# Down products of both feed-forward parts as seven block products for eight, added up in DRAM

## The chip, the core and the metric

The program runs on one core of a Trainium2 chip, as one launch. The metric is device time in microseconds (us) of that launch; lower is better. The engines that matter here are TensorE (PE in the profile; PEld is its weight load), VectorE (DVE), ScalarE (ACT), GpSimd (POOL) and SyncE (SP). SP and POOL issue the DMAs.

## The reference, cut to what matters

One layer of a streaming encoder, all in float32, with x of 1024 rows by 1024 features and a hidden width of 2816:

```python
def swiglu(h, w_gate, w_up, w_down):
    return (jax.nn.silu(h @ w_gate) * (h @ w_up)) @ w_down

    x = x + 0.5 * swiglu(rmsnorm(x, ffn1_norm[l]), ffn1_w_gate[l], ffn1_w_up[l], ffn1_w_down[l])
    x = x + hybrid_mixer(rmsnorm(x, mix_norm[l]), w_in[l], conv_w[l], conv_b[l],
                         sb_out_norm[l], conv_out_norm[l], w_out[l])
    x = x + 0.5 * swiglu(rmsnorm(x, ffn2_norm[l]), ffn2_w_gate[l], ffn2_w_up[l], ffn2_w_down[l])
    return rmsnorm(x, final_norm)
```

The change touches the last product of each `swiglu`, hidden (1024 x 2816) by `w_down` (2816 x 1024), once in part 1, before the mixer, and once in part 2, at the end.

## The kernel before

**Products in three.** A float32 product is made of three matmuls on operands that are split in a high and a low piece (hi by hi, hi by lo, lo by hi). `split` makes the high piece on ScalarE (a copy to the matmul's type, L169) and the low one on VectorE (a subtraction, L170). `mm3` issues the three matmuls, all from L91; one works on a 128 x 128 left tile and 512 columns, and adds up in a bank of PSUM.

**Gate and up.** The hidden tiles (22 of 128 rows, each in two halves of 512 columns) come from units. From tile 2 on a unit makes a tile's two products, gate and up, together as seven block products, named P1, P6, P2, P7, P5, Q4 and P3, in place of eight: the left blocks are combined on VectorE (`left`, L471 to L474), so are the right ones, once, and sums of the results on VectorE give the four blocks (L554 to L565). The hidden tile is written to DRAM, `h_sp`, by a DMA from POOL (L571).

**Down.** Hidden tiles are taken in 11 pairs. Down goes over 14 `TURNS`. A turn has an output tile row g, its partner g + 4, and a window of n pairs (1, 2, 3, then 4 eight times, then 3, 2, 1; 44 in all), so that pairs come and leave one by one while four groups of outputs take turns. In a turn, each pair takes 24 matmuls: two tile rows, two halves, two tiles, three matmuls. `down_prep` of the next turn runs between the products: it splits the pair that is new (1 MB: hidden tiles in part 1, rows of `w_down` in part 2; four splits of 512 columns) and the turn's own columns (rows of the other operand, in tiles named `w`). Both pass through one of two `raw` buffers of 1 MB; `L.load()` issues the next load on SP when one has been taken (L191).

**The flush.** At a turn's end `flush` adds the four banks to tiles of x (part 1, `to_mixer`, L766) or of the residual r (part 2, `to_output`, L1134), four operations on VectorE; these 16 tiles of 128 x 512 stay on chip all through down, after loads in the first four turns (L760, L1128). In the last four turns a tile is done: in part 1 it is fed to the mixer (`act1.feed`: a scaled split at L175 and L176, a running sum of squares at L268 and L269) and written to DRAM, while V, the first projection of the mixer, follows on TensorE; in part 2 the row is normalised (squares on ScalarE L1140, small sums L1143 and L1146, a power on POOL L1151, scaling L1155 and L1157) and written out.

**Order.** The code is written in the order above. The framework's scheduler gives each engine its own sequence and may move instructions ahead of others; waits between engines come from the tiles that they share and from buffers that come round (72 of the tiles named `s`, 10 of `w`, 2 of `raw`, 8 banks of PSUM).

## Time and profile before

| | |
|---|---|
| time, median of three runs | 1918.11 us (1917.59 to 1919.18) |
| time of the profiled execution | 1919.72 us |
| its span | 1918.0 us |
| TensorE busy | 98% of the span, 8440 matmuls |
| VectorE, ScalarE, GpSimd busy | 62%, 40%, 7% |
| TensorE's granted clock, mean | 0.99 |
| data moved by DMA | 187.07 MB, mean 98 GB/s |

The span runs from the first to the last instruction of the profiled execution; its own time stands beside it. An engine's share is an average over stages. In the rows further below a group is a line of the kernel, an engine, an operation and a shape, with its count, busy time and mean, and behind it the engine's idle time just before these instructions and what ended it.

### The profile page before, as it was taken

The numbers are of one execution on the slowest core, as the hardware profiler recorded it, in microseconds if no ns is written. First come the engines' busy times: TensorE is split into PE (matmuls) and PEld (weight loads), VectorE is DVE, ScalarE is ACT, GpSimd is POOL, SyncE is SP. The second block draws the span as 40 slices with busy tenths as digits, with TensorE's granted clock in tenths as the row PEclk, the third lists the DMA queues.
The fourth block names the chain that finished last, engine by engine and source line by source line (L and its number), as shares of the span: only waits on it lengthen the run. The fifth ranks groups of instructions, "written<-read, shape, count | busy, mean of one in ns | idle before, by whom it ended". The sixth has DMA issues, their size and how long they took to land.

```text
span 1918.0 us, 22275 instructions
## 1 busy us (share of the span) xinstructions
PE 1872.8 (98%) x8440; PEld 1549.3 (81%) x8440; DVE 1182.9 (62%) x1829; ACT 770.4 (40%) x1366; POOL 133.0 (7%) x238
## 2 busy tenths in 40 slices
PE   6989999999999999999999999999999999999997
PEld 5768888888888888888888877877888888888886
DVE  4896555655543258577788798679555656554324
ACT  4543222222321046466687785634223232232113
POOL 1100000000000011110101000200000000000001
PEclk8989999999999999999999999999999999999999
DMA  7123222223742032422313324303222322464202
GB/s 236 50 73 97 84 86 80 88 77 101 249 155 83 17 120 90 94 64 63 92 49 77 97 83 154 132 22 110 77 88 77 93 72 94 133 219 137 83 28 77
DMA packets 206907, 187.07 MB, mean 98 GB/s; under 512 B 8608, under 2 KB 174544, under 8 KB 206800
## 3 DMA queue, kind: packets, MB, share of 16 engines
q1 hardware_dynamic: 190160, 140.55, 24.4%
q0 software_dynamic: 16640, 45.10, 7.3%
q8 instruction: 66, 1.08, 0.2%
q14 instruction: 41, 0.34, 0.1%
HBM read 133.46 MB, written 42.73 MB: 92 GB/s over the span
## 4 chain that ended last, share of the span: by engine, by line
PE 91%; DVE 5%; issue 1%; ACT 1%; DMA 1%; SPq 0%; POOL 0%; POOLq 0%; DVEq 0%; ACTq 0%
PE ps L91 89%; DVE s L170 1%; DMA raw<-in_ffn_w_gate 1%; DVE w L170 1%; DVE s L269 0%; DVE s L496 0%; PE ps L277 0%; DVE s L595 0%; DVE s L176 0%; PE ps L853 0%; DMA s<-in_x 0%; SPq L677 0%; ACT w L169 0%; PE ps L683 0%; DVE s L875 0%
## 5 line engine op out<-in xcount | busy, mean ns | idle before, releaser
L91 PE MATMUL ps<-s,w 128*128 128x512 f32 x6880 | 1623.1, 391 | 25.9 <-ACT s L175 11.7
L91 PEld LDWEIGHTS ps<-s,w 128*128 128x128 f32 x6880 | 1286.0, 189 | 294.2 <-ACT s L175 12.6
L169 ACT CAST w<-raw 128x1024 fp32r<-128x1024 f32 (+3 forms) x182 | 181.1, 996 | 493.8 <-PE ps L91 339.6
L170 DVE TENSOR_TENSOR w<-raw,w 128x1024 fp32r<-128x1024 f32 (+3 forms) x182 | 209.2, 1151 | 138.4 <-ACT w L169 80.1
L91 PE MATMUL ps<-s,s 128*128 128x512 f32 (+3 forms) x704 | 179.0, 375 | 2.0 <-DVE s L170 1.0
L91 PEld LDWEIGHTS ps<-s,s 128*128 128x128 f32 x704 | 132.0, 188 | 29.3 <-DVE s L170 1.8
L170 DVE TENSOR_TENSOR s<-raw,s 128x512 fp32r<-128x512 f32 x128 | 85.0, 684 | 56.0 <-ACT s L169 56.0
L169 ACT CAST s<-raw 128x512 fp32r<-128x512 f32 x128 | 74.6, 617 | 85.0 <-DMA raw<-in_ffn_w_down 46.7
L566 ACT ACTIVATE s<-s 128x512 f32<-128x512 f32 x40 | 25.3, 633 | 202.8 <-DVE s L565 202.8
L766 DVE SCALAR_TENSOR_TENSOR s<-ps,s 128x512 f32<-128x512 f32 x56 | 38.0, 688 | 97.7 <-PE ps L91 97.3
L1134 DVE SCALAR_TENSOR_TENSOR s<-ps,s 128x512 f32<-128x512 f32 x56 | 37.9, 687 | 93.5 <-PE ps L91 93.4
L571 POOL DMA_DIRECT2D h_sp<-s x80 | 43.2, 539 | 742.7 <-DVE s L570 742.6
L551 ACT ACTIVATE s<-ps 128x512 f32<-128x512 f32 x40 | 23.8, 598 | 133.0 <-PE ps L91 133.0
L170 DVE TENSOR_TENSOR w<-w,w 128x1024 fp32r<-128x1024 f32 x40 | 49.0, 1224 | 41.2 <-PE ps L91 39.0
L471 DVE TENSOR_TENSOR w<-raw 128x1024 f32<-128x1024 f32 x40 | 48.8, 1223 | 34.6 <-PE ps L91 34.6
L554 DVE TENSOR_TENSOR s<-s,ps 128x512 f32<-128x512 f32 x40 | 27.4, 686 | 66.2 <-PE ps L91 66.2
L1007 DVE TENSOR_TENSOR s<-s,ps 128x128 f32<-128x128 f32 (+2 forms) x96 | 52.6, 548 | 16.8 <-ACT s L1003 16.4
L995 ACT ACTIVATE s<-ps 128x128 f32<-128x128 f32 (+2 forms) x96 | 47.0, 489 | 37.8 <-PE ps L91 37.5
L557 DVE TENSOR_TENSOR s<-s,ps 128x512 f32<-128x512 f32 x40 | 27.4, 686 | 56.3 <-PE ps L91 56.3
L170 DVE TENSOR_TENSOR s<-s,s 128x512 fp32r<-128x512 f32 x88 | 58.4, 682 | 5.6 <-ACT s L169 5.5
L1003 ACT ACTIVATE s<-s 128x128 f32<-128x128 f32 (+2 forms) x96 | 50.2, 523 | 20.6 <-DVE s L999 19.3
L169 ACT CAST s<-s 128x512 fp32r<-128x512 f32 x88 | 51.0, 618 | 18.5 <-DVE s L328 7.7
(122 smaller groups left out, 1451.8 us busy)
## 6 DMA issues: line engine op xcount, KB each, us to landing
h_sp<-s POOLq DMA_DIRECT2D x88, 256.0 KB, 2.3
raw<-in_ffn_w_gate SPq DMA_DIRECT2D x43, 512.0 KB, 3.9
raw<-in_ffn_w_up SPq DMA_DIRECT2D x43, 512.0 KB, 5.2
raw<-h_sp SPq DMA_DIRECT2D x11, 1024.0 KB, 5.0
raw<-in_ffn_w_down SPq DMA_DIRECT2D x11, 1024.0 KB, 4.8
raw<-in_w_in SPq DMA_DIRECT2D x20, 512.0 KB, 3.7
s<-s POOLq DMA_DIRECT2D x72, 128.0 KB, 2.4
x_sp<-s POOLq DMA_DIRECT2D x32, 256.0 KB, 2.3
```

The costliest lines, as they stand in the source:

```text
L91: nc.tensor.matmul(out, lhs, rhs, **kw)
L169: nc.scalar.copy(hi, x)
L170: nc.vector.tensor_tensor(out=lo, in0=x, in1=f(hi), op=ALU.subtract)
L471: nc.vector.tensor_tensor(out=two(y), in0=two(blk(1, 2)), in1=blk(3).unsqueeze(1).to_broadcast([P, 2, HALF]), op=ALU.add)
L554: nc.vector.tensor_tensor(out=self.u2, in0=self.p1, in1=o, op=ALU.subtract)
L557: nc.vector.tensor_tensor(out=self.u3, in0=self.u2, in1=self.o[2], op=ALU.add)
L571: nc.gpsimd.dma_start(out=self.out[:, hs(hf)], in_=u)
L766: nc.vector.scalar_tensor_tensor(out=x, in0=o[hf], scalar=0.5, in1=x, op0=ALU.mult, op1=ALU.add)
L995: behind(nc.scalar.activation(u["s"][:, cols], u["z"][:, cols], AF.Exp), table_set)
L1003: nc.scalar.activation(sc, sc, AF.Ln, bias=1.0)
L1007: nc.vector.tensor_tensor(out=sc, in0=sc, in1=u["z"][:, cols], op=ALU.max)
L1134: nc.vector.scalar_tensor_tensor(out=r, in0=o[hf], scalar=0.5, in1=r, op0=ALU.mult, op1=ALU.add)
```

## The change

Down becomes seven block products for eight in both parts, on the plan that gate and up had before. `h_sp` goes. In its place `Aside` takes hidden tiles as they are made and writes seven combinations for each pair of tiles to DRAM, `c_sp`: three are halves of the tiles as they stand, four are sums or differences; four operations on VectorE a pair (L637) and seven puts of 256 KB from POOL. In part 1 these are the right blocks and come back ready (`right_back`, L729), while the columns of `w_down` are combined into left blocks by `left`, now with a width. In part 2 they are the left blocks (`left_back`, L506: seven loads a turn, in rows of 128 columns), and the right ones are combined from rows of `w_down` (`right_rows`).

A turn runs the seven products in the order P1, P6, P2, P7, P5, Q4, P3, each n pairs deep: 21 matmuls a pair in place of 24. P1 and P2 share a bank, P7 and Q4, P5 and P3, so the second of each waits until the first has been taken out. The windows are now 2, 3, 4, 4, 3, 3, 3, 4, 4, 4, 4, 3, 2, 1 pairs, 44 as before. The first ten turns add four results each onto x or r in DRAM, by DMAs from POOL that accumulate (`add`, L795); one sum u stays on chip for each g (L805, L808). The last four turns load x or r back (four loads of 256 KB a turn) and add the results and u to it on VectorE (`end`, L835). The factor of a half is now in the hidden tile.

The diff, cut to its core (the parts on loads of weights and on the normalisation are left out):

```diff
--- before.py
+++ after.py
-    h_sp = [dr.tile([NF, P, S], F32, name=f"h_sp{i}") for i in range(2)]
...
-    TURNS = [(i % 4, max(0, i - 3), min(NQ, i + 1)) for i in range(NQ + 3)]
+    FACTORS = ("P2", "P1", "P3", "P6", "P7", "P5", "Q4")
+    c_sp = [dr.tile([7, NQ, P, HALF], F32, name=f"c_sp{i}") for i in range(2)]
+    UPTO = (2, 3, 4, 4, 5, 6, 7, 8, 9, 10) + (NQ,) * 4
+    TURNS = [(i % 4, UPTO[i - 4] if i > 3 else 0, n) for i, n in enumerate(UPTO)]
...
-    def left(raw):
+    def left(raw, n=HALF):
...
+    def left_back(g, q0, q1):
+        a = {}
+        n = (q1 - q0) * P
+        def load(to, i):
+            nc.sync.dma_start(out=to.rearrange("p (k c) -> p k c", c=P),
+                              in_=c_sp[1][i, q0:q1, :, g * P : (g + 1) * P].rearrange("k p c -> p k c"))
+        yield a
+        for i in (0, 2, 4):
+            raw = w4(F32)[:, : 2 * n]
+            for j in range(2):
+                load(raw[:, j * n : (j + 1) * n], i + j)
+            parts = split(w4()[:, : 2 * n], w4()[:, : 2 * n], raw)
+            for j in range(2):
+                a[FACTORS[i + j]] = tuple(x[:, j * n : (j + 1) * n] for x in parts)
+            yield
+        raw = s()[:, :n]
+        load(raw, 6)
+        a["Q4"] = split(s(F32R)[:, :n], s(F32R)[:, :n], raw)
...
+    class Blocks:
...
+        def product(self, name):
             i = BANK[name]
             first = i not in self.o
             if first:
                 self.o[i] = bank()
             o = self.o[i]
-            for k in range(4):
-                run(mm3(o, wk(self.a[name], k), self.b[name][k], first and k == 0,
-                        k == 3 and name in ("P2", "P6", "Q4", "P3"), skip_group_check=True))
+            for k in range(self.n):
+                run(mm3(o, wk(self.a[name], k), self.b(name, k), first and k == 0,
+                        k == self.n - 1 and name in ("P2", "P6", "Q4", "P3"), skip_group_check=True))
             self.done.add(name)
+            return o
...
+    class Aside:
...
+        def take(self, m, hf, x):
+            j, odd = divmod(m, 2)
+            if not odd:
+                if not hf:
+                    self.e0 = x
+                    self.put(j, 0, x)
+                else:
+                    self.e1 = x
+                    self.t1 = self.comb(s(), self.e0, x, self.op)
+                    self.put(j, 1, self.t1)
+            elif not hf:
+                self.o0 = x
+                self.put(j, 2, x)
+            else:
+                self.put(j, 3, x)
+                t2 = self.comb(s(), self.t1, x, ALU.add)
+                self.put(j, 5, t2)
+                t3 = self.comb(self.e1, x, self.e1, self.op)
+                self.put(j, 4, t3)
+                t4 = self.comb(s(), t2, self.o0, self.op)
+                self.put(j, 6, t4)
...
+    def right_back(q):
+        b = ring[q] = {}
+        def load(name):
+            raw = s()
+            nc.sync.dma_start(out=raw, in_=c_sp[0][FACTORS.index(name), q])
+            return raw
+        raw = load(FEW[0])
+        for i, name in enumerate(FEW):
+            now, raw = raw, load(FEW[i + 1]) if i < 6 else None
+            b[name] = split(s(F32R), s(F32R), now)
             yield
+    def right_rows(q):
+        b = ring[q] = {}
+        raw, _ = L.take()
...
+        done("P1", b11)
+        comb(b11, b11, b12, ALU.subtract)
+        t2 = comb(s(), b11, b22, ALU.add)
+        yield
+        done("P6", t2)
+        yield
+        done("P2", b21)
+        comb(b21, t2, b21, ALU.subtract)
+        yield
+        done("P7", comb(b12, b22, b12, ALU.subtract))
+        yield
+        done("P5", b11)
+        yield
+        done("Q4", b21)
+        yield
+        done("P3", b22)
         L.load()
-    def down(flush, start=None):
+        yield
+    def down_prep(i, j):
+        g, q0, q1 = TURNS[j]
+        steps = [left_back(g, q0, q1) if i else left(L.take()[0], (q1 - q0) * P)]
+        lefts[j] = next(steps[0])
+        steps += [(right_rows if i else right_back)(q) for q in news(j)]
+        while steps:
+            for x in list(steps):
+                if next(x, steps) is steps:
+                    steps.remove(x)
+            yield
+    class Turn(Blocks):
...
+        def add(self, i, hf, x):
+            nc.gpsimd.dma_start(out=self.acc(self.g + 4 * i, hf), in_=x, accum_op=ALU.add)
+        def do(self, name, ready):
+            o = self.product(name)
+            if name == "P1":
+                if self.first:
+                    self.kept[self.g] = s()
+                    nc.scalar.copy(self.kept[self.g], o)
+                else:
+                    u = self.kept[self.g]
+                    nc.vector.tensor_tensor(out=u, in0=u, in1=o, op=ALU.add)
+            if name == "P6":
+                u = self.kept[self.g]
+                nc.vector.tensor_tensor(out=u, in0=u, in1=o, op=ALU.subtract)
+            if self.last:
+                self.end(name, o, ready)
+                return
+            if name == "P2":
+                x = s()
+                nc.scalar.copy(x, o)
+                self.add(0, 0, x)
+            if name == "P7":
+                self.p7 = s()
+                nc.scalar.activation(self.p7, o, AF.Copy, scale=-1.0)
+            if name == "P5":
+                nc.vector.tensor_tensor(out=self.p7, in0=self.p7, in1=o, op=ALU.subtract)
+                self.add(1, 1, self.p7)
+            if name == "Q4":
+                x = s()
+                nc.scalar.activation(x, o, AF.Copy, scale=-1.0)
+                self.add(1, 0, x)
+            if name == "P3":
+                x = s()
+                nc.scalar.copy(x, o)
+                self.add(0, 1, x)
+        def end(self, name, o, ready):
+            x = lambda i, hf: self.tiles(self.g + 4 * i, hf)
+            def comb(t, y, op):
+                nc.vector.tensor_tensor(out=t, in0=t, in1=y, op=op)
+            if name == "P6":
+                u = self.kept.pop(self.g)
+                comb(x(0, 1), u, ALU.add)
+                comb(x(1, 1), u, ALU.subtract)
+                comb(x(1, 0), u, ALU.subtract)
+            if name == "P2":
+                comb(x(0, 0), o, ALU.add)
+                ready(self.g, 0)
+            if name == "P7":
+                comb(x(1, 1), o, ALU.subtract)
+            if name == "P5":
+                comb(x(1, 1), o, ALU.subtract)
+                ready(self.g + 4, 1)
+            if name == "Q4":
+                comb(x(1, 0), o, ALU.subtract)
+                ready(self.g + 4, 0)
+            if name == "P3":
+                comb(x(0, 1), o, ALU.add)
+                ready(self.g, 1)
+    def down(i, acc, tiles, back, ready):
         for j, (g, q0, q1) in enumerate(TURNS):
-            prep = down_prep(j + 1) if j + 1 < len(TURNS) else iter(())
-            if start:
-                start(j)
-            last = j >= NQ - 1
-            for i in range(2):
-                o = [bank(), bank()]
-                n = (q1 - q0) * 2
-                for k in range(n):
-                    hi, lo = (a[:, k * P : (k + 1) * P] for a in rows_of[j][i])
-                    for hf in range(2):
-                        run(mm3(o[hf], (hi, lo), ring[q0 + k // 2][k % 2, hf], k == 0, k == n - 1))
-                    if k % 2:
-                        next(prep, None)
-                flush(j, g, i, o)
+            prep = down_prep(i, j + 1) if j + 1 < len(TURNS) else iter(())
+            if j + 1 >= NQ - 1 and j + 1 < len(TURNS):
+                for hf in range(2):
+                    back((j + 1) % 4, hf)
+                    back((j + 1) % 4 + 4, hf)
+            turn = Turn(j, acc, tiles)
+            for name in FEW:
+                turn.do(name, ready)
+                next(prep, None)
             run(prep)
         ring.clear()
-        rows_of.clear()
+        lefts.clear()
     x_in = t["x"][0]
...
-    def x_back(j):
-        if j < 4:
-            for i in range(2):
-                for hf in range(2):
-                    d = j + 4 * i
-                    nc.sync.dma_start(out=xT(d, hf), in_=x_sp[0][d][:, hs(hf)])
-
-    def to_mixer(j, g, i, o):
-        d = g + 4 * i
-        for hf in range(2):
-            x = xT(d, hf)
-            nc.vector.scalar_tensor_tensor(out=x, in0=o[hf], scalar=0.5, in1=x, op0=ALU.mult, op1=ALU.add)
-            if j >= NQ - 1:
-                act1.feed(d, hf, x, x)
-                nc.gpsimd.dma_start(out=x_sp[1][d][:, hs(hf)], in_=x)
-
-    down(to_mixer, x_back)
+    def x_back(d, hf):
+        nc.sync.dma_start(out=xT(d, hf), in_=x_sp[0][d][:, hs(hf)])
+    def to_mixer(d, hf):
+        x = xT(d, hf)
+        act1.feed(d, hf, x, x)
+        nc.gpsimd.dma_start(out=x_sp[1][d][:, hs(hf)], in_=x)
+    down(0, lambda d, hf: x_sp[0][d][:, hs(hf)], xT, x_back, to_mixer)
...
```

How the change moves instructions, at three places. The first is VectorE in the last turn but one and the last turn of part 1's down. In before, four flushes a turn alternate with the mixer's feed (L176) and sums (L269):

```order
L176 SCALAR_TENSOR_TENSOR s_4982<-s_3416,gains_495,s_4981 128x512
L766 SCALAR_TENSOR_TENSOR s_3481<-ps_4992,s_3481 128x512
L176 SCALAR_TENSOR_TENSOR s_4988<-s_3418,gains_495,s_4987 128x512
L766 SCALAR_TENSOR_TENSOR s_3483<-ps_4993,s_3483 128x512
L269 TENSOR_TENSOR s_4716<-s_4716,s_5004 128x512
L269 TENSOR_TENSOR s_4718<-s_4718,s_5007 128x512
L176 SCALAR_TENSOR_TENSOR s_5014<-s_3481,gains_495,s_5013 128x512
L766 SCALAR_TENSOR_TENSOR s_3485<-ps_5024,s_3485 128x512
L176 SCALAR_TENSOR_TENSOR s_5020<-s_3483,gains_495,s_5019 128x512
```

In the changed kernel the same place, around the first products of the last turn (`s_3746` is the sum u, `ps_5565` the bank of P1 and P2, `ps_5570` that of P6, `ps_5590` that of P7 and Q4, `ps_5598` that of P5 and P3):

```order
L805 TENSOR_TENSOR s_3746<-s_3746,ps_5565 128x512
L269 TENSOR_TENSOR s_5231<-s_5231,s_5572 128x512
L808 TENSOR_TENSOR s_3746<-s_3746,ps_5570 128x512
L835 TENSOR_TENSOR s_5446<-s_5446,ps_5565 128x512
L835 TENSOR_TENSOR s_5450<-s_5450,s_3746 128x512
L835 TENSOR_TENSOR s_5452<-s_5452,s_3746 128x512
L835 TENSOR_TENSOR s_5448<-s_5448,s_3746 128x512
L176 SCALAR_TENSOR_TENSOR s_5586<-s_5446,gains_495,s_5585 128x512
L269 TENSOR_TENSOR s_5278<-s_5278,s_5592 128x512
L835 TENSOR_TENSOR s_5452<-s_5452,ps_5590 128x512
L170 TENSOR_TENSOR w_5652<-raw_5410,w_5651 128x1024
L835 TENSOR_TENSOR s_5452<-s_5452,ps_5598 128x512
```

Ten evictions and adds stand where four flushes stood, and the feed of a tile (L176) follows only when its last add is made; in part 2 the same adds stand before the normalisation.

The second place is SP's queue at the start of part 2's down in the changed kernel (`raw` are rows of `w_down`, `c_sp_80` the combinations; x2 marks two alike):

```order
L191 DMA raw_13659<-in_ffn_w_down 128x2x1024
L191 DMA raw_13793<-in_ffn_w_down 128x2x1024
L506 DMA w_13844<-c_sp_80 128x2x128 x2
L506 DMA w_13879<-c_sp_80 128x2x128 x2
L506 DMA w_13908<-c_sp_80 128x2x128 x2
L506 DMA w_14051<-c_sp_80 128x3x128 x2
L506 DMA s_13940<-c_sp_80 128x2x128
L506 DMA w_14073<-c_sp_80 128x3x128 x2
L191 DMA raw_14030<-in_ffn_w_down 128x2x1024
L191 DMA raw_14036<-in_ffn_w_down 128x2x1024
```

The third load of down weights, `raw_14030`, stands behind the left loads of turn 0 and the first of turn 1, and there are two `raw` buffers. In before, the second operand's loads went through `raw` too.

The third place is TensorE's sequence at the start of part 1's down in the changed kernel (`ps_3736`, `ps_3760`, `ps_3803` and `ps_3825` are turn 1's banks of P1, P6, P7 and P5, `ps_3607` is turn 0's bank of P1 and P2):

```order
L91 MATMUL ps_3736<-s_3417,w_3616 128x512
L91 MATMUL ps_3736<-s_3418,w_3616 128x512
L91 MATMUL ps_3736<-s_3417,w_3617 128x512
L91 MATMUL ps_3760<-s_3441,w_3655 128x512
L91 MATMUL ps_3760<-s_3442,w_3655 128x512
L91 MATMUL ps_3803<-s_3502,w_3674 128x512
L91 MATMUL ps_3760<-s_3441,w_3656 128x512
L91 MATMUL ps_3760<-s_3447,w_3655 128x512
...
L91 MATMUL ps_3803<-s_3503,w_3674 128x512
L91 MATMUL ps_3825<-s_3537,w_3674 128x512
L91 MATMUL ps_3825<-s_3538,w_3674 128x512
L91 MATMUL ps_3607<-s_3471,w_3401 128x512
L91 MATMUL ps_3607<-s_3472,w_3401 128x512
```

Products of turn 1 stand ahead of turn 0's P2; in before the turns followed one another there as they are written.

## Rows read from the trace of the kernel before

**Rows 1.** The page: span, engines' busy time, the chain that ended last.
```profile
span 1918.0 us, 22275 instructions
...
PE 1872.8 (98%) x8440; PEld 1549.3 (81%) x8440; DVE 1182.9 (62%) x1829; ACT 770.4 (40%) x1366; POOL 133.0 (7%) x238
...
PE 91%; DVE 5%; issue 1%; ACT 1%; DMA 1%; SPq 0%; POOL 0%; POOLq 0%; DVEq 0%; ACTq 0%
```

**Rows 2.** Windows, down at 482:726, 1670:1910; us, busy (count), PEclk, DMA share, GB/s.
```profile
97.00:470.00 373.00, 367.29 (x1602) 302.46 (x1601) 238.34 (x311) 112.43 (x157) 20.50 (x38) 0.99 0.28 84
482.00:726.00 244.00, 244.00 (x1078) 202.06 (x1077) 108.29 (x152) 66.66 (x100) 9.63 (x20) 1.00 0.38 123
1285.00:1660.00 375.00, 370.41 (x1627) 304.83 (x1628) 236.04 (x307) 115.30 (x163) 20.50 (x38) 1.00 0.27 84
1670.00:1910.00 240.00, 236.27 (x1043) 195.31 (x1041) 100.50 (x160) 58.76 (x104) 7.83 (x9) 1.00 0.36 115
```

**Rows 3.** Groups by form, 482:726 us, down of part 1.
```profile
L766 DVE SCALAR_TENSOR_TENSOR s<-ps,s 128x512 f32<-128x512 f32 x56 | 38.0, 688 | 97.7 <-PE ps L91 97.3
L170 DVE TENSOR_TENSOR w<-raw,w 128x1024 fp32r<-128x1024 f32 x21 | 25.6, 1222 | 11.8 <-ACT w L169 11.8
L170 DVE TENSOR_TENSOR s<-raw,s 128x512 fp32r<-128x512 f32 x39 | 25.4, 684 | 22.9 <-ACT s L169 22.9
...
L169 ACT CAST s<-raw 128x512 fp32r<-128x512 f32 x38 | 21.5, 616 | 38.3 <-DMA raw<-h_sp 38.3
...
L176 DVE SCALAR_TENSOR_TENSOR s<-s,gains,s 128x512 fp32r<-128x512 f32 x15 | 10.8, 745 | 0.0
...
L269 DVE TENSOR_TENSOR s<-s,s 128x512 f32<-128x512 f32 x12 | 7.7, 683 | 0.0
...
L170 DVE TENSOR_TENSOR w<-raw,w 128x768 fp32r<-128x768 f32 x4 | 3.8, 956 | 3.3 <-ACT w L169 3.3
...
L170 DVE TENSOR_TENSOR w<-raw,w 128x256 fp32r<-128x256 f32 x2 | 0.8, 416 | 0.0
```

**Rows 4.** Timeline from 690 us, end of part 1's down: start, us, instruction.
```profile
719.71 9.23 PE L91 MATMUL ps<-w,s 128*128 128x512 f32 x40
...
729.33 1.05 PE L277 MATMUL ps<-ones_r,s 128*128 128x1 f32 x8 [0.39 <-DVE s L269]
```

**Rows 5.** Timeline from 1885 us, the kernel's end.
```profile
1884.80 21.47 PE L91 MATMUL ps<-s,w 128*128 128x512 f32 x94
...
1908.85 0.15 DVE L1146 SCALAR_TENSOR_TENSOR sm<-sm,sm 128x1 f32<-128x1 f32 x1
...
1909.08 0.92 POOL L1151 TENSOR_TENSOR sm<-sm,mhalf 128x1 f32<-128x1 f32 x1 [2.30 <-DVE sm L1146]
1910.04 0.72 ACT L1157 ACTIVATE s<-s,sm 128x512 f32<-128x512 f32 x1 [1.28 <-POOL sm L1151]
1910.04 0.49 DVE L1155 TENSOR_SCALAR s<-s,sm 128x512 f32<-128x512 f32 x1 [0.44 <-POOL sm L1151]
```

**Rows 6.** Groups by form, 200:455 us, gate and up of part 1.
```profile
L471 DVE TENSOR_TENSOR w<-raw 128x1024 f32<-128x1024 f32 x13 | 15.9, 1225 | 14.0 <-PE ps L91 14.0
...
L473 DVE TENSOR_TENSOR raw<-w,raw 128x512 f32<-128x512 f32 x13 | 8.9, 684 | 0.0
```

**Rows 7.** DMA issues: count, KB each, median us to landing.
```profile
h_sp<-s POOLq DMA_DIRECT2D x88, 256.0 KB, 2.3
...
raw<-in_ffn_w_down SPq DMA_DIRECT2D x11, 1024.0 KB, 4.8
...
s<-x_sp SPq DMA_DIRECT2D x32, 256.0 KB, 5.1
raw<-in_ffn_w_down SPq DMA_DIRECT2D x16, 512.0 KB, 5.3
raw<-h_sp SPq DMA_DIRECT2D x16, 512.0 KB, 5.8
```

**Rows 8.** Timeline from 455 us, SP's queue.
```profile
474.68 1.92 SPq L760 DMA_DIRECT2D s<-x_sp  x4
```

More of the change, by code (lines that the diff above doesn't have):

```diff
@@ L386, in ffn_weights @@
             yield [part(j * S, w[:, m * P : (m + 1) * P]) for j, w in enumerate((wg, wu))]
[L387 to L388 removed]
         for j, (g, q0, q1) in enumerate(TURNS):
[L390 to L393 removed]
+            if i:
+                for q in news(j):
+                    yield [part(0, wd[2 * q * P : 2 * (q + 1) * P])]
+                continue
+            n = (q1 - q0) * P
+            rows = wd[2 * q0 * P : 2 * q1 * P].rearrange("(k two p) c -> two p k c", two=2, p=P)
+            yield [(b * n, n, (lambda a: a.rearrange("p (k c) -> p k c", c=P)),
+                    rows[two, :, :, d * P : (d + 1) * P])
+                   for b, (two, d) in enumerate(((1, g), (0, g), (1, g + 4), (0, g + 4)))]
     def mixer_weights():
@@ L601, in gate_up @@
         preps = [left(L.take()[0]) for _ in range(2)]
-        units = [Unit(next(p), b, out[nstd + j]) for j, p in enumerate(preps)]
+        units = [Unit(next(p), b, out(nstd + j)) for j, p in enumerate(preps)]
         for p in preps:
@@ L616, in gate_up @@
         for m in range(nstd + 2, NF):
-            unit = Unit(a, b, out[m])
+            unit = Unit(a, b, out(m))
             if m + 1 < NF:
@@ L621, in gate_up @@
             else:
-                prep = down_prep(0)
+                prep = down_prep(i, 0)
             for name in FEW:
@@ L626, in gate_up @@
             run(prep)
-    ring, rows_of = {}, {}
-    def down_prep(j):
-        if j < NQ:
-            raw, _ = L.take()
-            ring[j] = {}
-            for i in range(4):
-                ring[j][divmod(i, 2)] = split(s(F32R), s(F32R), raw[:, hs(i)])
-                yield
-            L.load()
-        raw, n = L.take()
-        rows_of[j] = []
-        for i in range(2):
-            c = slice(i * n // 2, (i + 1) * n // 2)
-            rows_of[j].append(split(w4()[:, : n // 2], w4()[:, : n // 2], raw[:, c]))
-            yield
-        L.load()
@@ L647, in down @@
[L647 to L663 removed]
+    ring, lefts = {}, {}
@@ new lines, in right_back, with comb, done @@
+    def right_back(q):
[8 more added lines that the diff above has]
+            b[name] = split(s(F32R), s(F32R), now)
+            yield
+    def right_rows(q):
+        b = ring[q] = {}
+        raw, _ = L.take()
+        b11, b12, b21, b22 = (raw[:, i * HALF : (i + 1) * HALF] for i in range(4))
+        def comb(out, x, y, op):
+            nc.vector.tensor_tensor(out=out, in0=x, in1=y, op=op)
+            return out
+        def done(name, x):
+            b[name] = split(s(F32R), s(F32R), x)
+        done("P1", b11)
[14 more added lines that the diff above has]
+        done("P3", b22)
+        L.load()
+        yield
@@ new lines, in down_prep, with __init__ @@
+    def down_prep(i, j):
[7 more added lines that the diff above has]
+                    steps.remove(x)
+            yield
+    class Turn(Blocks):
+        kept = {}
+        def __init__(self, j, acc, tiles):
+            self.g, q0, q1 = TURNS[j]
+            super().__init__(lefts[j], lambda name, k: ring[q0 + k][name], q1 - q0)
+            self.first, self.last = q0 == 0, q1 == NQ
+            self.acc, self.tiles = acc, tiles
+        def add(self, i, hf, x):
+            nc.gpsimd.dma_start(out=self.acc(self.g + 4 * i, hf), in_=x, accum_op=ALU.add)
+        def do(self, name, ready):
+            o = self.product(name)
+            if name == "P1":
[52 more added lines that the diff above has]
+                ready(self.g, 1)
```

128 lines of the change are left out of this document (69 added, 59 removed).

## The prediction

> **What bounds the kernel now.** I read first the shares of the engines and the chain of work that ended last: TensorE is busy 98% of the 1918.0 us, and 91% of the chain is TensorE [rows 1]. Then the stretches the change touches, by windows: in both down products TensorE is busy 240 to 244 us of 240 to 244, at a granted clock of 1.00, with VectorE at 108 and 100 us, ScalarE at 67 and 59 and the DMA engines at 0.36 to 0.38 [rows 2]. So down waits for nothing but its own matmuls, and a matmul costs 244.00/1078 = 0.2263 us in part 1 and 236.27/1043 = 0.2265 in part 2: 0.2264 us. Grouped by form, VectorE's flushes idle 97.3 us behind TensorE [rows 3]; it has room on the mean. Last the two ends. After the last down product of part 1 TensorE runs 40 matmuls of the V projection, and the next product that needs VectorE starts 0.39 us after them [rows 4]: the handover is covered almost exactly. At the kernel's end the last matmul stops at 1884.80 + 21.47 = 1906.27, and the last normalisation at 1910.76 [rows 5].
>
> The profiled execution took 1919.72 us for the span of 1918.0; the median of the three runs is 1918.11, so I sum on the profile and take 1.6 off at the end. These three differ by 1.6 us; 0.2% (3.8 us) is about what a measurement tells from no change: faster is below 1914.3, slower above 1921.9.
>
> **Removed.** Down of a part had 14 turns with 24 matmuls per pair of hidden tiles, 44 pair-turns: 1056. Seven products for eight make 21, so 924. Two parts save 264 matmuls: 264 × 0.2264 = **−59.8 us**. That is all if TensorE stays fed. A turn of n pairs is then 4.75 n us and one product 0.68 n us; down of a part falls from 239 to 209 us. The 112 flushes of 0.688 us [rows 3] go too, but they were hidden.
>
> **Added, and hidden in the middle.** Counting the order's VectorE instructions in down of part 1 at the durations of [rows 3] gives some 185 us in 210, in the middle turns 77 to 80%; ScalarE some 110. Neither binds on the mean; both bind where work is bunched, which is at the ends of the two downs. Four combinations of 512 columns per pair are added on VectorE in gate_up, 0.684 each as the row of that shape has it [rows 6], 2.7 us per pair of 38 us, where VectorE now runs 238.34/373 = 64% [rows 2]: 72%, hidden under TensorE but for jitter, **+1** (0 to 2). The three puts more per pair are POOL's and not waited for.
>
> **End of part 1's down.** The four end turns add onto the residual on VectorE: ten operations a turn, as the order piece on VectorE shows, plus the feeding of the mixer. Between the eviction of P1 of turn 12 and that of P5 of turn 13 (P3 shares its bank and waits) VectorE has 36 instructions: 18 evictions and adds at 0.686, 6 feeds at 0.745, 6 sums at 0.683, splits of 1.222, 2 × 0.416 [rows 3], and three of 128 columns, by the slope (0.684 − 0.416)/256 an estimated 0.28 each: 12.4 + 4.5 + 4.1 + 1.2 + 0.8 + 0.8 = 23.8 us. TensorE has 54 matmuls and five of V that stand ahead: 59 × 0.2264 = 13.4. It waits **+10.4**. The last V matmuls behind hide the rest as now [rows 4]. Bounds: 6, if the earlier work is drawn forward, and 14.
>
> **End of part 2's down.** The same stretch: 24 adds and scalings of 0.686, six small ones at 0.15, three scalings at 0.49 [rows 5], splits 3 × 0.416 + 0.28 [rows 3]: 20.4 us against 54 × 0.2264 = 12.2, so 8.2 late. In return the last chain, 4.5 us from the last matmul on [rows 5], loses one flush of two, since P3's half row alone is left behind it: about 0.7 to 0.9 less. Net **+7.5** (4 to 11).
>
> **Start of part 1's down.** The left factors of turn 1 are built in tiles that the last unit's P3 frees. From there to the split that gives P3 and P6 of turn 2 the order has 31 VectorE instructions: eleven splits of 512 columns at 0.684, two of 768 at 0.956, two of 1024 at 1.222, three operations of 384 columns at 0.55 (on the same slope), two combinations of 768 and 1024 at 0.96 and 1.23 [rows 3, 6], and eleven combinations and evictions of 512 columns at 0.686: 23.2 us, against 85 matmuls or 19.2. So 4.0 late; the shuffling of turns 0 and 1, seen in the order piece on TensorE, is counted in the 85. The transfers say much the same: the last unit and turns 0 and 1 carry 28 loads of 7.3 MB, left columns of 2.4, puts of 1.3 and adds of 2.1, 13.1 MB in 42.8 us, 306 GB/s; the present stretches move 84 at a share of 0.28, 123 at 0.38 and 115 at 0.36, so 300 to 324 when all engines work [rows 2]. That just fits, up to 1 late; adds counted twice make 15.2 MB, 50.7 us at 300, 8 late. I take **+6** (3.6 to 10.6, both waits in part).
>
> **Start of part 2's down.** There are two raw buffers. As the order piece on SP shows, the third load of down weights stands behind the left loads and waits for a buffer: it is free only after pair 0's last split, 7.8 us of VectorE after the last unit's Q4 starts. Then come 4.8 for 1 MB [rows 7], a cast of 0.62 and a subtraction of 0.69 [rows 3]: 4.4 late for turn 1's P1, 6.2 for its P6. **+6.5** (4 to 10). The loads of the residual are moved from the turns 0 to 3 to the turns 10 to 13; on SP each takes 0.48 us of issue [rows 8], four a turn, in turns of 14 to 19 us: nothing.
>
> **Adds in DRAM.** Forty DMAs per part of 256 KB, issued by POOL at 0.54 us each, add onto DRAM. No row shows one. From below a plain write of 256 KB, landed in 2.3 us; from above its read and write, 5.1 + 2.3 = 7.4 [rows 7]. No engine waits for one but for its buffer, a turn later; what counts is the DMA engines' time. In part 1 a turn of three pairs (14.3 us) moves 1.8 MB of right blocks, 0.8 of left and 1.05 of adds: 3.7 MB, 12.2 us at 300 GB/s; adds counted twice make 4.7 MB, 15.7 us, 1.4 late in each of three turns. Turns of four pairs have 19.0 us for 13.1 or 16.6; part 2 carries 5% less. **+2** (0 to 7) for both parts, nearer the read-and-write bound, since an add must do both.
>
> The Trainium skill, "DMA: Bandwidth & Descriptors", section "Bandwidth", speaks against this: transfers of 64 KB reach 138 GB/s and one should batch to 1 MiB, and part 2's left factors now come in loads of 128 to 256 KB with rows of 512 bytes. In the trace 512-byte rows cost little: 512 KB, issued in pairs, land in 5.3 and 5.8 us, 1 MB in long rows in 4.8 [rows 7]. At 138 GB/s throughout, a turn of three pairs in part 2 would take an estimated 25 us for 14.3; by the rows 12.
>
> **Sum.** −59.8 + 1 + 10.4 + 7.5 + 6 + 6.5 + 2 = −26.4: 1919.7 − 26.4 = 1893.3, on the median 1891.7; I write **1893**, since small waits at the seams are likelier missed than double counted.
>
> **Rivals.**
> A, the forecast: the give-backs of 33 us, each with its own bounds, come to 18 at the lowest and 55 at the highest; together 22 to 45 are likely: 1880 to 1903. 0.62.
> B, the ends are filled: two thirds of the 30 us at the four ends vanish, since work is pulled forward into them (five V matmuls and the shuffled turns show that the order does it): −59.8 + 12 = −48, so 1870 (1865 to 1880). For it: VectorE idles 97 us in a down now [rows 3]. Against: at the ends its work hangs on the products just made. 0.15.
> C, the other side: the DMA engines become the bound in down. At four plain writes for an add, a turn of three pairs carries 2.6 + 4.2 = 6.8 MB, 23 us for 14.3, one of four 7.1 MB, 24 for 19: 3 × 8 + 3 × 5, and turns 0 to 2 some 25 more, 62 a part, of which buffers absorb perhaps a third: −26 + 2 × 41 = +56, 1974. At three writes the same sum gives 5 us, 1 us and 8 in those turns, 26 a part, two thirds of it 17: −26 + 34 = +8. So it decides from about three plain writes an add. For it: no row prices an add. Against: a read and a write land in 7.4, which is 3.2 of 2.3 but mostly time of travel [rows 7]. 0.12. In its section "Rules for kernel authors" the page named above says that an accumulating DMA reads its destination and writes it later, so that another write between is lost and each must wait for the one before; adds to one block stand four turns apart here, so that alone costs nothing.
> D, the change keeps next to nothing: each end at its upper bound gives back 45 to 60, so 1903 to 1921. 0.08.
> E, part 2's left loads, now in rows of 512 bytes and 128 to 256 KB, move slowly. At a quarter of 300 GB/s a turn of three pairs takes 3.5/0.3 = 11.6 us, and 7.9 more for its 0.8 MB: 19.5 for 14.3; one of four 12.5 and 10.5 more, 23 for 19: 3 × 5 + 4 × 4, 31 us, 1912 to 1925; at a half it all fits. For it: each turn has seven such loads. Against: such rows land in 5.3 to 5.8 us for two of 512 KB together [rows 7]. 0.03. That is the mechanism of the page's rule on 64 KB, at a rate below its 138.
>
> **Chances.** Faster is A, B and 0.04 of D: 0.81; same the rest of D and 0.02 of E: 0.06; slower C and the rest of E: 0.13. The range leaves out C, E, a third of D and a sliver of B, 0.2 in all: 1868 to 1914.
>
> **What the profile after would show.** TensorE with 264 matmuls fewer, still 0.226 us each, and in four places stalls: before P3 of the last turn of part 1's down with VectorE as releaser (about 10 us), the same at the kernel's end (8), at turn 1 of part 1 behind a split or a c_sp load (6), at turn 1 of part 2 behind a load of down weights (6). The middle turns show TensorE at over 97%; a plain write and an adding one would differ in time to landing by at most 5 us. I am wrong if the middle turns stall with DMA as releaser (C), if the stalls at the ends add up to less than 12 (B), or if gate_up takes over 3 us more.

## The result, and the profile after

The changed kernel takes 1949.24 us (median of four runs, 1944.06 to 1956.14), before 1918.64 (1917.59 to 1919.99): 1.0161 times as long, 95% interval 1.0126 to 1.0196. That is 31 us longer, well outside the scatter of the runs, where 25 us less were forecast. The profiled execution took 1946.61 us; its span is 1944.9, 26.9 more than before, and the accounts below are made on it.

The page after: the span, the engines' busy time and count, and the two DMA queues with packets, MB and the time of their packets as a share of 16 engines.

```profile
span 1944.9 us, 23049 instructions
...
PE 1845.2 (95%) x8176; PEld 1506.7 (77%) x8176; DVE 1384.8 (71%) x2145; ACT 887.6 (46%) x1576; POOL 238.2 (12%) x384
...
q1 hardware_dynamic: 216720, 157.87, 26.8%
q0 software_dynamic: 33440, 83.38, 16.6%
```

Against [rows 1]: 8440 − 8176 = 264 matmuls are gone, as planned, and TensorE's share of the span fell from 98% to 95%. The second queue, POOL's, stood at this in before:

```profile
q0 software_dynamic: 16640, 45.10, 7.3%
```

Where the time went is read off TensorE's timeline. The product Q4 has both operands in tiles `s`, so in the timeline it stands out as `ps<-s,s`. From the order of TensorE's instructions I count the matmuls between two such marks; at 0.2264 us each they give the time that TensorE needs, and what the trace has beyond that is lost. Here are the marks in the changed kernel: the last unit but one of gate and up, turns 3, 11 and 13 of part 1's down, the mixer's first sum (L277); then the same of part 2 without the sum. Below, the start of a down is what lies between the unit's mark and turn 3's, the middle runs from turn 3 to turn 11, and the end is the rest.

```profile
460.01 2.88 PE L91 MATMUL ps<-s,s 128*128 128x512 f32 x12
...
549.62 2.88 PE L91 MATMUL ps<-s,s 128*128 128x512 f32 x12
...
699.06 2.20 PE L91 MATMUL ps<-s,s 128*128 128x512 f32 x9
...
724.68 1.62 PE L91 MATMUL ps<-s,s 128*128 128x512 f32 x3 [4.58 <-DVE s L835]
...
737.13 1.05 PE L277 MATMUL ps<-ones_r,s 128*128 128x1 f32 x8
...
1659.48 2.88 PE L91 MATMUL ps<-s,s 128*128 128x512 f32 x12
...
1760.10 2.88 PE L91 MATMUL ps<-s,s 128*128 128x512 f32 x12
...
1905.28 2.20 PE L91 MATMUL ps<-s,s 128*128 128x512 f32 x9
...
1933.27 1.65 PE L91 MATMUL ps<-s,s 128*128 128x512 f32 x3 [1.74 <-DVE s L835]
```

Between the first two marks stand 357 matmuls, 80.8 us; the trace has 89.6, so 8.8 are lost at the start of part 1's down. From turn 3 to turn 11 it is 594 matmuls, 134.5 us, for 149.4: 15.0 lost in the middle. Part 2 has the same counts: 100.6 for 80.8, 19.8 lost at its start, and 145.2 for 134.5, 10.7 in its middle. The sum at L277 stood at 729.33 in before [rows 4], so part 1 as a whole lost 7.8; its unit of 460.01 stood at 455.87, so 4.1 of these were gone before down began. From L277 to the unit of 1659.48 are 922.35 us, in before 912.94: 9.4 more are lost ahead of part 2's down. The mixer in between took 0.2 more, so they belong to gate and up. The ends are not measured by themselves: they are what is left of the 26.9. All of it beside the forecast, in us:

| step of the prediction | forecast | in the trace |
|---|---|---|
| matmuls removed | −59.8 | −59.8 |
| gate and up (both) | +1 | +13.5 |
| start of part 1's down | +6 | +8.8 |
| middle turns of both parts, adds in DRAM | +2 | +25.7 |
| end of part 1's down | +10.4 | +9.8 |
| start of part 2's down | +6.5 | +19.8 |
| end of part 2's down, net | +7.5 | +9.1 |
| sum | −26.4 | +26.9 |

The middle turns. The issues of DMAs, with count, KB each and median us to landing:

```profile
s<-c_sp SPq DMA_DIRECT2D x83, 256.0 KB, 6.4
x_sp<-s POOLq DMA_DIRECT2D x72, 256.0 KB, 4.1
...
raw<-in_ffn_w_down SPq DMA_DIRECT2D x11, 1024.0 KB, 7.7
```

40 of the 72 writes to `x_sp` add, and the median of all is 4.1 us where plain ones took 2.3; the 1 MB load, 4.8 in [rows 7], takes 7.7. What follows from late loads is seen at 590 us, in turn 6 (start, us, engine, instruction, idle time before and its releaser):

```profile
592.42 6.53 SPq L729 DMA_DIRECT2D s<-c_sp  x7
...
600.14 0.62 ACT L169 CAST s<-s 128x512 fp32r<-128x512 f32 x1 [8.90 <-DMA s<-c_sp]
...
600.79 0.69 DVE L170 TENSOR_TENSOR s<-s,s 128x512 fp32r<-128x512 f32 x1 [6.66 <-ACT s L169]
...
603.23 0.51 PE L91 MATMUL ps<-s,w 128*128 128x512 f32 x1 [3.36 <-ACT s L169]
```

Seven loads are issued in a burst; ScalarE stands 8.90 us before the first has landed, with casts and evictions queued behind; VectorE waits for ScalarE and TensorE for both. The DMA engines are full in that burst and nearly idle after it (us, busy and count of PE, PEld, DVE, ACT, POOL, then the granted clock, DMA share, GB/s; a share over 1 says that packets' times overlap):

```profile
594.00:598.00 4.00, 4.00 (x19) 3.30 (x19) 0.14 (x1) 0.00 (x0) 0.00 (x0) 1.00 1.12 262
...
602.00:606.00 4.00, 1.75 (x4) 1.24 (x5) 4.00 (x5) 4.00 (x7) 0.58 (x1) 0.82 0.11 39
```

The start of part 2's down, on SP, ScalarE and TensorE:

```profile
1693.22 1.84 SPq L191 DMA_DIRECT2D raw<-in_ffn_w_down  x2
...
1700.16 0.62 ACT L169 CAST s<-raw 128x512 fp32r<-128x512 f32 x1 [8.05 <-DMA raw<-in_ffn_w_down]
...
1700.83 1.95 PE L91 MATMUL ps<-s,w 128*128 128x512 f32 x3 [4.14 <-ACT s L169]
```

The third load of down weights goes out at 1693.22, when the raw buffer is free, and lands 6.9 us later. The left loads (L506) were held back too: in this stretch (1660 to 1715 us) SP stood 32.0 us, in six waits, until TensorE had read tiles `w` that they were to overwrite.

```profile
SPq L506 <- PE ps L91: 32.0, 6, 8.3
```

After the stall three matmuls take 1.95 us, not 0.68. The windows show the clock that TensorE was granted:

```profile
710.00:730.00 20.00, 13.21 (x45) 9.51 (x45) 19.75 (x33) 9.22 (x14) 4.24 (x8) 0.76 0.44 147
1700.00:1720.00 20.00, 15.69 (x49) 10.61 (x50) 11.50 (x17) 9.92 (x17) 3.50 (x4) 0.74 0.85 201
...
1701.00:1710.00 9.00, 6.24 (x12) 3.44 (x13) 5.67 (x9) 4.02 (x7) 0.90 (x1) 0.50 0.80 206
...
1920.00:1940.00 20.00, 9.87 (x29) 6.25 (x28) 15.61 (x35) 8.07 (x21) 3.69 (x4) 0.72 0.30 105
530.00:670.00 140.00, 130.40 (x558) 104.86 (x559) 88.57 (x123) 67.51 (x112) 26.84 (x31) 0.99 0.79 201
```

After the 4.14 us in which TensorE stood before 1700.83, it was granted 0.50 of its clock from 1701 to 1710: the lower level, 1.2 GHz of 2.4. In 1700 to 1720 it is busy 15.69 us for 49 matmuls, 4.6 more than 49 × 0.2264. And at the end of part 1's down VectorE is busy 19.75 us of 20 and TensorE 13.21: that is the wait that was worked out ahead.

Gate and up. At the start of part 2's, on VectorE, first before (L170 on `s<-s` splits the right factors, L579 ends the second hidden tile), then after (L671 and L637 are that tile and its combinations):

```profile
1271.36 1.28 DVE L170 TENSOR_TENSOR s<-s,s 128x512 fp32r<-128x512 f32 x2
...
1278.69 1.28 DVE L579 TENSOR_TENSOR s<-s,ps 128x512 f32<-128x512 f32 x2 [2.44 <-PE ps L91]
```

```profile
1286.71 1.28 DVE L671 SCALAR_TENSOR_TENSOR s<-s,ps 128x512 f32<-128x512 f32 x2 [7.26 <-PE ps L91]
...
1289.05 1.89 DVE L637 TENSOR_TENSOR s<-s,s 128x512 f32<-128x512 f32 x3
...
1290.85 1.28 DVE L170 TENSOR_TENSOR s<-s,s 128x512 fp32r<-128x512 f32 x2
...
1291.59 4.63 PE L91 MATMUL ps<-s,w 128*128 128x512 f32 x10 [2.98 <-DVE s L170]
```

Before, the splits stood ahead of the hidden tile and ran under its matmuls. After, the hidden tile comes first in VectorE's order; VectorE idles 7.26 us until TensorE has made it, with the splits queued behind, and then TensorE waits for them. So VectorE had the time; it had the wrong operation next.

### The profile page after: what moved, and what is told of

Read it like the earlier page. It is cut to its first block, busy times and chain, and to the rows that moved or that the text cites. A ratio compares the mean times of both kernels' runs of the same rounds, so it can differ in the third digit from the quotient of the medians.

```text
span 1944.9 us, 23049 instructions
## 1 busy us (share of the span) xinstructions
PE 1845.2 (95%) x8176; PEld 1506.7 (77%) x8176; DVE 1384.8 (71%) x2145; ACT 887.6 (46%) x1576; POOL 238.2 (12%) x384
## 3 DMA queue, kind: packets, MB, share of 16 engines
q0 software_dynamic: 33440, 83.38, 16.6%
## 5 line engine op out<-in xcount | busy, mean ns | idle before, releaser
L91 PE MATMUL ps<-s,w 128*128 128x512 f32 x6352 | 1533.2, 395 | 72.0 <-ACT s L169 19.7
L91 PEld LDWEIGHTS ps<-s,w 128*128 128x128 f32 x6352 | 1192.6, 190 | 339.4 <-ACT s L169 24.5
L170 DVE TENSOR_TENSOR w<-raw,w 128x1024 fp32r<-128x1024 f32 (+3 forms) x154 | 181.6, 1180 | 110.9 <-PE ps L91 61.3
L91 PE MATMUL ps<-s,s 128*128 128x512 f32 (+3 forms) x968 | 246.6, 382 | 14.0 <-DVE s L835 8.5
L634 POOL DMA_DIRECT2D c_sp<-s x154 | 83.5, 542 | 782.4 <-DVE s L620 618.7
L170 DVE TENSOR_TENSOR w<-w,w 128x1024 fp32r<-128x1024 f32 (+3 forms) x96 | 104.6, 1090 | 95.4 <-PE ps L91 48.6
L170 DVE TENSOR_TENSOR s<-s,s 128x512 fp32r<-128x512 f32 (+2 forms) x190 | 125.7, 676 | 58.0 <-ACT s L169 56.9
L169 ACT CAST s<-s 128x512 fp32r<-128x512 f32 (+2 forms) x190 | 111.4, 611 | 73.5 <-DMA s<-c_sp 45.9
L169 ACT CAST w<-w 128x1024 fp32r<-128x1024 f32 (+3 forms) x96 | 90.1, 938 | 98.4 <-DMA w<-c_sp 86.6
L170 DVE TENSOR_TENSOR s<-raw,s 128x512 fp32r<-128x512 f32 (+2 forms) x120 | 78.5, 672 | 13.0 <-ACT s L169 12.7
L601 ACT ACTIVATE s<-ps 128x512 f32<-128x512 f32 x40 | 23.8, 598 | 122.8 <-PE ps L91 122.8
L169 ACT CAST s<-raw 128x512 fp32r<-128x512 f32 (+2 forms) x120 | 70.7, 607 | 8.1 <-DMA raw<-in_ffn_w_down 8.1
L637 DVE TENSOR_TENSOR s<-s,s 128x512 f32<-128x512 f32 x88 | 56.8, 687 | 1.3
```

Source lines behind the costliest of these rows:

```text
L91: nc.tensor.matmul(out, lhs, rhs, **kw)
L169: nc.scalar.copy(hi, x)
L170: nc.vector.tensor_tensor(out=lo, in0=x, in1=f(hi), op=ALU.subtract)
L634: nc.gpsimd.dma_start(out=self.sp[FACTORS.index(self.names[i]), j], in_=x)
L637: nc.vector.tensor_tensor(out=out, in0=x, in1=y, op=op)
```

## The experiments

Each was run against before on the same chip (before took 1918.94 to 1919.66 on the three chips used). Differences named below are to the changed kernel's own median of 1949.24, whose runs scatter over 12 us, so they are good to a few us. What a place lost is read from one trace a run. Two theories stood at first. Q: loads are issued too late, because of SP's order and the two raw buffers. T: the DMA engines' time that the adds take.

**Adds as plain writes.**

```diff
-            nc.gpsimd.dma_start(out=self.acc(self.g + 4 * i, hf), in_=x, accum_op=ALU.add)
+            nc.gpsimd.dma_start(out=self.acc(self.g + 4 * i, hf), in_=x)
```

> The 80 adding DMAs write without adding (so ten turns' results replace x and r in place of being added). Theory Q (loads are issued too late: SP's queue and the two raw buffers hold back the c_sp loads, and ScalarE's casts, in order, hold back evictions): the stalls stay, 0 to 12 us faster than the changed kernel. Theory T (the DMA engines' time of the adds is what costs): the adds take twice a plain write's time on the queue's share, so halving it gives most of the 25 us lost in the middle turns back, 20 to 35 us faster.

1927.11 us, 1.0038 of before (1.0025 to 1.005): 22 less than the changed kernel. The middles lose 4.7 and 3.1 us in place of 15.0 and 10.7. In nine traces that have the adds and 68 or 72 tiles `s`, the changed kernel's among them, the middles lose 13.3 to 18.6 and 10.7 to 14.1, so this lies well outside.

```profile
q0 software_dynamic: 28320, 83.38, 12.7%
...
s<-c_sp SPq DMA_DIRECT2D x83, 256.0 KB, 5.5
x_sp<-s POOLq DMA_DIRECT2D x72, 256.0 KB, 2.9
```

**No adds.** The line above is left out.

> The 80 adding DMAs are left out altogether (ten turns' results are dropped). Theory Q: at most 15 us faster than the changed kernel, with stalls before turns whose c_sp loads stand behind a load that waits for a raw buffer still there. Theory T: 30 us or more faster, middle turns of both parts free of stalls.

1920.07 us, 1.0001 (0.9992 to 1.001): 29 less. The middles lose 0.8 and 1.4 us.

```profile
q0 software_dynamic: 21920, 62.41, 9.8%
...
s<-c_sp SPq DMA_DIRECT2D x83, 256.0 KB, 5.0
```

```profile
530.00:670.00 140.00, 139.71 (x616) 115.00 (x615) 100.47 (x140) 72.88 (x120) 1.08 (x2) 1.00 0.50 162
```

The same stretch has TensorE busy 139.71 of 140 us, with the loads, the queues and the two raw buffers as they were. SP waits no less for the raw buffers than in the changed kernel (482 to 700 us, the changed kernel first, then without adds):

```profile
SPq L191 <- DVE s L170: 112.1, 12, 13.1
...
SPq L191 <- DVE s L170: 132.0, 13, 13.0
```

So T holds for the middles, though 29 us fall just short of the 30 that it asked for, and Q, which allowed 15 at most, does not. The price of an add follows from the queue's shares of the three spans: 0.166 × 1944.9 = 322.9 us of the engines' time with adds, 0.127 × 1925.4 = 244.5 with plain writes, 0.098 × 1916.4 = 187.8 without. 80 plain writes (20.97 MB) take 56.7, 80 adds 135.1: 2.4 plain writes an add. The loads' own queue, q1, took about the same in all three (521, 529 and 527 us), so a load that lands later was not moved more slowly; this speaks for loads that wait their turn behind the adds.

An add has a second way to cost time: its tile `s` stays taken until it has landed, and a c_sp load may need that tile. SP did stand for it twice in part 1's down, and as long with plain writes (482 to 700 us, the changed kernel first):

```profile
SPq L729 <- DMA x_sp<-s: 8.9, 2, 5.0
...
SPq L729 <- DMA x_sp<-s: 8.7, 2, 5.6
```

So the held tile does not explain what plain writes gave back. For the 4 us of part 1's middle that only the run without adds gave back, no run takes the two ways apart.

Even without adds the kernel is no faster than before: the two gate and ups, the starts and the ends give the whole gain back by themselves.

**The left load behind the c_sp loads**, in part 1:

```diff
-        L.load()
+        (load or L.load)()
...
+            if owed and k == 3:
+                L.load()
```

> In part 1's down, the load of left columns into a raw buffer is issued a few products later, behind the c_sp loads of the next turn, so that SP does not wait for the raw buffer with c_sp loads queued behind it. Theory Q: 10 to 20 us of part 1's 24 us at its start and middle come back. Theory T: within 5 us of the changed kernel, since the bytes are the same.

1950.04 us, 1.0164 (1.0138 to 1.019): no change. Start and middle of part 1 lose 6.6 and 17.0, together 23.6, where it was 23.8. But the edit did not bring about the order that it was made for. The scheduler still put the left loads ahead of most of a turn's c_sp loads, and SP still stood 106.2 us for the raw buffers in 482 to 700 us (112.1 in the changed kernel):

```profile
545.00 1.98 SPq L191 DMA_DIRECT2D raw<-in_ffn_w_down  x4
547.07 5.03 SPq L729 DMA_DIRECT2D s<-c_sp  x7
```

So this run says nothing about Q. What speaks against Q as the cause for the middles is the run without adds; whether loads issued earlier would help beside the adds stays untested.

**No combinations in gate and up.**

```diff
-                t2 = self.comb(s(), self.t1, x, ALU.add)
-                self.put(j, 5, t2)
+                self.put(j, 5, x)
```

(and so for the other three)

> The four combinations per pair in gate and up are not made; tiles are put as they are in their place. Theory: the 13 us lost at the two starts of gate and up come from these operations and the buffers they hold; 9 to 14 us faster, units still 19.04 us. Rival: the starts are late for another reason (other order of the scheduler): under 4 us.

1937.87 us, 1.0094 (1.0068 to 1.0121): 11 less. Part 1's unit is 1.8 us ahead of before (454.10 for 455.87), part 2's 1.9 behind after its own L277 is allowed for: of 13.5 us, 0.2 is left. The splits stand ahead of the hidden tile (here L667) again, as in before:

```profile
1276.06 1.28 DVE L170 TENSOR_TENSOR s<-s,s 128x512 fp32r<-128x512 f32 x2
...
1283.39 1.28 DVE L667 SCALAR_TENSOR_TENSOR s<-s,ps 128x512 f32<-128x512 f32 x2 [2.44 <-PE ps L91]
```

**Combinations later.** Those of the first two pairs are made after the first two units (`late`), the rest as they were. In this version the halves of the second pair come in another order and are mixed up in the combinations, so the output is not the reference's; the work is the same.

```diff
         x_tiles.clear()
+        out.late()
         prep = left(L.take()[0])
```

> The combinations of the first two pairs of hidden tiles are made after the first two units, in place of among the splits of the right factors. Theory (they stand before the splits on VectorE): the 13 us lost at the two starts of gate and up fall to 2 to 4, 9 to 11 us faster, as without combinations (11). Rival (tiles held longer delay the right factors all the same): under 4 us.

1940.17 us, 1.0106 (1.008 to 1.0132): 9 less. 0.2 and 4.2 us are left of the 4.1 and 9.4, and here too the splits stand ahead of the hidden tile. So the loss lay in VectorE's order at one place, not in the sum of the operations: the units' pace is 19.04 us with and without. Why the scheduler chose that order was not looked into. The sizes are rough: over the nine traces with the combinations at their old place the unit of part 1 stands at 457.7 to 461.1 and the way from L277 to that of part 2 takes 918 to 926 us; over the three without them or with them later, 453.6 to 456.1 and 915 to 919.

A part of the 9.4 is the clock. At this place TensorE was granted 0.83 in the changed kernel and 1.00 without combinations (0.84 with them later):

```profile
1290.00:1310.00 20.00, 14.98 (x49) 10.87 (x49) 12.77 (x20) 8.06 (x14) 1.63 (x3) 0.83 0.12 46
...
1290.00:1310.00 20.00, 16.64 (x69) 12.76 (x70) 17.83 (x28) 12.24 (x22) 0.00 (x0) 1.00 0.00 0
```

**Three raw buffers, twelve tiles w, and both.** Paid for with 4, 4 and 8 of the 72 tiles `s`.

```diff
-        return sb.tile([P, HALF], dt, name=nm("s"), tag="s", bufs=72)
+        return sb.tile([P, HALF], dt, name=nm("s"), tag="s", bufs=68)
...
-            raw = sb.tile([P, 2 * S], F32, name=nm("raw"), tag="raw", bufs=2)
+            raw = sb.tile([P, 2 * S], F32, name=nm("raw"), tag="raw", bufs=3)
```

> Three raw buffers in place of two, paid for with four of the 72 tiles of 128 x 512. Theory (the third load of down weights waits for pair 0's last split): the 14 us lost at the start of part 2's down fall to under 5, 8 to 12 us faster in all. Rival (the start is late since ring and left tiles are built just in time, whatever the load): under 4 us; four tiles fewer may cost up to 5.

1939.44 us, 1.0105 (1.009 to 1.012): 10 less, as forecast, but not where it was forecast: the 14 us fall to 11.5, and the start of part 1's down, not meant, falls from 8.8 to 5.2.

> Twelve tiles named w in place of ten, paid for with four of 72 tiles of 128 x 512. If the left loads of part 2 wait mostly for w tiles that TensorE still reads, the 10 us of its middle turns fall by 4 to 8. If the adds' time on the DMA engines is the cause, as the runs without adds say, under 3.

1940.47 us, 1.0111 (1.0096 to 1.0126): 9 less.

> Three raw buffers and twelve tiles w together, with 64 tiles of 128 x 512 in place of 72. Theory (the start of part 2's down stands behind two locks in a row, the raw buffer and the tiles w that TensorE still reads): its 14 us at turn 0's Q4 fall under 6, where each alone left 9 to 12. Rival (something else is late there): 9 or more. The middle turns may get slower, since the ring then has fewer tiles.

1961.45 us, 1.0223 (1.02 to 1.0246): 12 more. Turn 0's Q4 of part 2, 13.9 us late in the changed kernel, is 11.5 late with three raw buffers, 9.1 with twelve w and 2.5 with both; so two locks, the raw buffer and the tiles w, stand there in a row, as the third expectation had it, and the first, which gave one lock the whole, was wrong in size. Not all of it is gained: up to turn 1's Q4 6.8 us are then lost in place of 1.8, and the start as a whole loses 12.6 in place of 19.8. What makes the rest was not tried. With 64 tiles `s` the middle of part 1 loses 36 us in place of 15, where the runs with 68 lose 15.2 to 17.5; that the four tiles fewer did it is likely, but no run takes them away alone. Twelve w left part 2's middle at 11.5, so its w tiles are not what holds it.

**Two of three sums of u on GpSimd**, in the end turns:

```diff
-                comb(x(0, 1), u, ALU.add)
+                comb(x(0, 1), u, ALU.add, nc.gpsimd)
...
-                comb(x(1, 0), u, ALU.subtract)
+                comb(x(1, 0), u, ALU.subtract, nc.gpsimd)
```

> In the last four turns two of the three operations that add u to the residual go from VectorE to GpSimd. Theory (VectorE has 10 us more than TensorE between P1 of turn 12 and P5 of turn 13): six operations of 0.69 fewer in that stretch, 3 to 4 us faster at each end, 6 to 8 in all. Rival (the end waits for a chain of one product's eviction, whoever does it): within 2 us or slower.

1952.24 us, 1.0178 (1.0163 to 1.0193): no gain. The trace shows the reason:

```profile
720.85 2.94 POOL L835 TENSOR_TENSOR s<-s,s 128x512 f32<-128x512 f32 x2 [2.44 <-issue]
721.23 1.43 DVE L835 TENSOR_TENSOR s<-s,s 128x512 f32<-128x512 f32 x1
...
722.58 2.29 DVE L170 TENSOR_TENSOR w<-raw,w 128x1024 fp32r<-128x1024 f32 x1
...
724.93 1.65 PE L91 MATMUL ps<-w,s 128*128 128x512 f32 x3 [6.08 <-DVE w L170]
```

While GpSimd runs its two, VectorE's operation takes 1.43 us, not 0.68, and the next 2.29, not 1.22: what was moved came back as longer operations on VectorE. The rival's number came (within 2 us or slower), but not its chain behind one product, as the next run shows.

**No sums of u.**

```diff
-                comb(x(0, 1), u, ALU.add)
-                comb(x(1, 1), u, ALU.subtract)
-                comb(x(1, 0), u, ALU.subtract)
```

> The three operations a turn that add u to the residual in the last four turns are left out (u is lost from the outputs). If VectorE's count sets the end of part 1's down, nine operations of 0.69 in the stretch of turns 11 to 13 give 4 to 6 us there; at the end of part 2, where the trace shows TensorE also waiting 5 us for left loads, 2 to 4; 6 to 10 us faster than the changed kernel. If the end waits for the chain behind one product, under 2.

1940.25 us, 1.0107 (1.009 to 1.0124): 9 less. From turn 12 to turn 13 part 1 loses 3.4 in place of 7.2, part 2 5.6 in place of 8.4. VectorE's count sets the end, in part 1 above all.

**Combinations later and three raw buffers**, a whole kernel:

> A whole kernel: the combinations of the first two pairs after the first two units, and three raw buffers. The two gains add up if each is at its own place: 16 to 20 us faster than the changed kernel, 1928 to 1934, still slower than before by 10 or more, since the adds and the ends stay.

1929.96 us (1920.09 to 1936.58), 1.0054 (1.0036 to 1.0072): 19 less, as the two gains add up; still slower than before.

## Why the prediction was wrong

**Right.** The 264 matmuls and their 59.8 us. The end of part 1's down: 10.4 forecast, 9.8 in the trace, with VectorE at 19.75 of 20 us as the cause. That of part 2: 7.5 and 9.1; part of it is another wait, ScalarE standing 5.68 us for a left load:

```profile
1923.52 0.41 ACT L169 CAST w<-w 128x256 fp32r<-128x256 f32 x1 [5.68 <-DMA w<-c_sp]
```

The start of part 1's down: 6 and 8.8. With three raw buffers it loses 3.6 less, but TensorE's order changes with them, as it did in the run with the left load moved, which loses 2.2 less. What sets the rest was not tried.

**Wrong, "Adds in DRAM": +2, and 25.7.** This is the largest miss. The price was nearly right, 2 plain writes in the sum and 2.4 measured. What failed is how it was turned into time: the DMA engines were taken as a pipe that costs nothing until it is full, so 15.7 us of transfers in a turn of 14.3 made 1.4. In the trace the share was 0.79 on the mean of 530 to 670 us, and the middles lost nearly thirteen times the forecast. The sum spread a turn's transfers over the whole turn. But the loads of a turn go out in a burst, just ahead of their use, and there the engines are full, 1.12 from 594 to 598, and at 0.11 eight us later. A c_sp load then lands after 6.4 us (median) and not after 5.0, and ScalarE, which casts in order, holds back the evictions behind it. Rival C had the DMA engines as the bound, from about three plain writes an add, but it too reckoned by whole turns, over which the engines had room. They were the bound in bursts, at 2.4 writes. That the middle turns stall behind DMA was one of the forecast's own signs of being wrong.

**Wrong, "Start of part 2's down": +6.5, and 19.8.** The place and the first lock, the raw buffer, were right; at 4.8 us the load was priced as in [rows 7], and landed in 6.9. Not seen was the second lock: the left loads wait for tiles w that TensorE still reads. Only with both opened do the 13.9 us at turn 0's Q4 fall to 2.5. Even then the start loses 12.6, about twice the forecast, and the cause of that stays open.

**Wrong, "Added, and hidden in the middle": +1, and 13.5.** The busy share (64%, then 72%) was right: 263.88 of 373 us in the changed kernel's 97 to 470 us, 71%, and the units' pace did not move. But the sum was made on a mean. At the start of gate and up the hidden tile, which has to wait for TensorE, and its combinations stood in front of the splits that the next product needs. The order of VectorE, which was read for the ends of down, was not read for this place. That gate and up took over 3 us more was another of these signs.

**Not in the sum at all: the clock.** In the two downs six windows of 20 us with a granted clock of 0.72 to 0.91 follow stalls; TensorE's busy time in them exceeds its matmuls at 0.2264 by 16.6 us in all (1700 to 1720: 4.6), and the window at the start of part 2's gate and up by 3.9. The clock cost at most about that much there, since some of these matmuls ran while other work was waited for. These us lie in the terms above, in the starts and ends most; the forecast had every matmul at 0.2264.

## What to carry to other kernels

A saving on the engine that bounds a kernel is worth what the seams let through: work out the order of the helping engines at each place where a phase starts or ends, and don't read a mean share there. Traffic that fits the DMA engines on the mean still costs time when it falls into a burst and delays loads that are issued just ahead of their use and cast by an engine that also empties PSUM; measure it by leaving the transfer out, which takes one run. And when SBUF is full, ask of each queue of buffers what it waits for: one more buffer opens one lock only.

## What the runs showed of the hardware

An accumulating DMA of 256 KB onto DRAM takes 2.4 times the engines' time of a plain one (6.4 us of all sixteen engines for a MB, against 2.7). It lands after 5.4 us, the plain one in its place after 3.1 (medians), and POOL spends 0.87 us on its issue (median; 0.54 on that of a plain one).

VectorE's operations on two SBUF operands of 512 columns get longer beside a GpSimd operation of the same kind: where GpSimd's had begun first, 0.68 us became 1.18 to 1.80 (six cases, beside GpSimd operations of 1.26 to 1.98). Those with one operand in PSUM stayed at 0.67 to 0.69. The Trainium skill, "SBUF — State Buffer", section "SBUF: two separate sides", says that the two share one pair of ports, locked for a whole instruction; the trace agrees.

The changed kernel's times scatter over 12 us between runs (1944 to 1956), those of before over 2.4. What differs between the runs was not looked into.
